# Attention phase of a one-core decoder layer: scaling of A's queries on VectorE, late stores, sample queries and sample transposes traced later, sample stream weighted 315 for 280

## The chip, the cores and the metric

The kernel is one launch on one core of a Trainium2 chip. The core has a matrix engine (PE, with its weight loads shown as PEld), a vector engine (DVE), a scalar engine (ACT) and a general engine (POOL), which run their own instruction lists in order and wait for one another by semaphores; SP only issues DMAs here, and ACT and POOL issue some too. The metric is the device time of one execution in microseconds (us); lower is better.

## What is computed

One decoder layer for a prompt of 1024 tokens and a sample group of 8 sequences with 4 new tokens each, over 1024 cached tokens in pages of 128. The reference, cut to its frame:

```python
def project(xn, w_in, pos, ...):          # one input projection, split by columns
    aq, ak, av, bq, bk, bv, iq, ik, iw = split(xn @ w_in)
    aq = rope(rms_norm(aq), pos); ak = rope(rms_norm(ak), pos)
    bq = rope(rms_norm(bq), pos); bk = rope(rms_norm(bk), pos)
...
a_out = dsa_attention(aq, iq, iw, ik, ...)   # A: 8 heads of 64, keys chosen by an indexer
b_out = diff_attention(bq, bk, bv, pos, lam) # B: 4 heads, softmax 1 - lam * softmax 2
b_out = rms_norm(b_out, subln) * (1.0 - lam_init)
h = x + concat(a_out, b_out) @ w_out
y = h + hier_moe(rms_norm(h))                # 32 experts, 2 chosen of one group of 8
```

The prompt attends to itself; the sample attends to its cached pages and its own new keys. Outputs are y for both groups and the new keys and values.

## The kernel before

The program runs in five stages, in this order: the input projection by sections of 512 columns (the last is AQ, the queries of A), with the indexer's selection among them; the head of the attention, in which the first tiles are loaded and turned; the attention; the output projection with the routing; and the experts. The prompt is cut into 8 tiles of 128 tokens, the sample is one tile of 32 rows.

**A section's end.** `evac` takes a tile's 512 columns out of PSUM. For queries and keys it copies them (ACT, `raw`), squares them, applies the rotary table (`rope`: one product on POOL, `m`, line 340, the other product and the sum on DVE, lines 342 and 343), computes the reciprocal root of the mean square (lines 348 to 352), and multiplies by it (line 387: `outs` or `outl`, by `rk`). For the query sections, prompt tiles only, line 387 is on POOL (line 386 chooses the engine); all others are on DVE. The result goes to the scratch tensor s_qa or s_qb by `store`, which keeps a few stores back in the list `late`. The last stores of AQ (tiles 6 and 7, named `outl`, two each) are still in `late` when the projection is over.

**The attention.** Two generators are interleaved by `mix`: `prompt_attention`, which goes through the 8 tiles of B and then of A, and `samples`, which does the sample's B, its A, and then the loading and splitting of w_out. Each yields the work that it has just traced as a number; `mix` always advances the one whose sum, divided by its total, is smaller. Both totals are 280. So the order on each engine is fixed by the order of tracing, and within it each engine waits for what it needs.

*Prompt.* `prep` loads a tile's keys and queries (kn, qn), splits them in two fp32r parts (kst, qh and ql), turns them (line 404), loads its values (VV, line 916) and turns its keys (line 920). For each of four pairs of heads (index u), `scores` makes the two score blocks (lines 936 and 937 on PE, 938 on DVE with the mask and the minimum, 940 the exponential on ACT), and normalises (for B lines 950, 954, 955 on DVE, which leave one block; for A line 958 on POOL). One round behind, `turned` turns the exponentials (PE line 876, then a copy `aT`), and another behind, `values` multiplies them with VV (lines 974 and 978). The list `late` is written out after tile 0 is prepared and before the loop over the tiles (lines 1039 to 1041), with `issue_after(holds[1])`, which puts the issue behind the given instruction.

*Sample.* `sample_attention` loads its queries and keys, turns them (lines 1080 and 1081, eight small transposes), clears QB on POOL (line 1083), copies the turned queries into it (line 1086, eight copies on DVE) and the keys to KN (line 1089). Then, for two groups of 4 sequences: for four chunks, it gathers 4 pages of keys (line 554, POOL), turns them (line 1104), and multiplies them with QB (line 1112); it makes the scores of the new keys (line 1120), takes the maximum, and the exponentials on ACT (line 1151 for the past, line 1152 for the new keys); it turns the exponentials (line 876 through `transposed`, from the tile sc, and line 1157), and multiplies them with 4 x 4 pages of values (line 1165). So the turn of the exponentials occurs four times: twice for B, twice for A.

After both generators, lines 1280 to 1283 split the sample's mixture mixS into a rounded part and a rest (msh, msl), which the output projection (lines 1325 to 1327) multiplies with w_out, the sample's tile first among its users.

## Time and profile before

| | |
|---|---|
| median of 3 runs | 1397.38 us (1395.25 to 1399.51) |
| the profiled execution | 1403.95 us, of it the profiled span 1402.1 us |
| PE busy in the span | 1265.0 us, 90% |
| DVE, ACT, POOL busy | 792.0 (56%), 561.5 (40%), 447.8 us (32%) |
| stage, from the span's start | projection to 466 us, head of the attention to 500 us, attention to 932 us, output projection to 1061 us, experts to 1402 us |
| PE in the output projection | 129.00 us busy of 129 |

The busy share of an engine says how much it does; which of its waits sets the end is read from the waits and the chain. In the rows further on, an instruction's line is that of the kernel before, `out<-in` are names of the program, a bracket at the end of a row is the time that the engine stood idle before it and what ended that, and PEclk is the share of full speed that the clock of PE was granted.

### The profile page before, as it was taken

The page shows a single profiled execution, that of the slowest core. Times are in us where ns is not written, and L with a number is a line of the kernel's source. Part 1 is how long each engine was busy: PE and PEld are TensorE (multiplying, and loading weights), DVE is VectorE, ACT ScalarE, POOL GpSimd, SP SyncE. Part 2 cuts the span into 40 slices and gives each one's busy share as a digit, 9 for nine tenths or more (in the row PEclk, how much of TensorE's full clock was granted, in tenths as well). Part 3 has the DMA queues.
Part 4 walks back from the last instruction along what each step waited for, and adds up shares of the span by engine and source line. Part 5 has one row for each costly group of instructions (what it writes and reads, how often), then busy time and mean ns, then how long its engine had stood idle before and what let it go on. Part 6 is the DMA issues. An engine that isn't in the chain of part 4 may idle for free.

```text
span 1402.1 us, 24778 instructions
## 1 busy us (share of the span) xinstructions
PE 1265.0 (90%) x9359; PEld 855.0 (61%) x9359; DVE 792.0 (56%) x2218; ACT 561.5 (40%) x1239; POOL 447.8 (32%) x505
## 2 busy tenths in 40 slices
PE   7999999997799689898889989999996999999994
PEld 4877675875467576776675776768884333333341
DVE  5544996969987677766655556946754111111110
ACT  5533666895432365544345555732220111111110
POOL 1012233254336534435236544321212112222101
PEclk9999999998899899999899999999997999999997
DMA  6223004133325765666467654347657999999992
GB/s 234 77 88 109 25 24 121 48 109 82 90 97 147 227 244 213 234 210 230 152 227 252 222 161 148 103 135 306 247 172 256 341 370 377 377 381 386 378 340 47
DMA packets 114149, 279.92 MB, mean 200 GB/s; under 512 B 50664, under 2 KB 50920, under 8 KB 101736
## 3 DMA queue, kind: packets, MB, share of 16 engines
q1 hardware_dynamic: 81248, 180.84, 35.4%
q0 software_dynamic: 26272, 95.43, 21.8%
q10 hardware_dynamic: 6504, 2.01, 0.6%
q8 instruction: 75, 1.23, 0.3%
q14 instruction: 50, 0.41, 0.1%
HBM read 234.33 MB, written 43.92 MB: 198 GB/s over the span
## 4 chain that ended last, share of the span: by engine, by line
PE 44%; DMA 9%; DVE 6%; issue 5%; POOL 3%; ACT 2%; SPq 0%; another core or an unknown queue 0%; POOLq 0%; ACTq 0%; DVEq 0%
PE acc L1513 9%; PE S L1533 4%; DMA wg<-in_w_exp_up_dram 4%; PE tr L1104 4%; PE tr L876 3%; PE acc L1325 3%; PE acc L1326 2%; PE acc L1327 2%; PE tr L1112 2%; PE own L1165 2%; PE acc L978 2%; DMA wg<-in_w_exp_gate_dram 2%; PE acc L974 2%; PE tr L936 2%; PE tr L937 2%
## 5 line engine op out<-in xcount | busy, mean ns | idle before, releaser
L532 PE MATMUL acc<-wh,xh 128*128 128x512 f32 x432 | 174.9, 405 | 15.3 <-ACT wh L508 15.3
L1513 PE MATMUL acc<-wg,xT 128*32 128x512 f32 x1536 | 174.7, 598 | 2.8 <-DMA wg<-in_w_exp_up_dram 2.4
L533 PE MATMUL acc<-wh,xl 128*128 128x512 f32 x432 | 172.1, 398 | 0.0
L940 ACT ACTIVATE mk<-mk,mx 128x256 f32<-128x256 f32 (+7 forms) x128 | 99.0, 775 | 83.4 <-DVE mx L938 74.0
L535 PE MATMUL acc<-wl,xh 128*128 128x512 f32 x320 | 126.6, 396 | 0.0
L1513 PEld LDWEIGHTS acc<-wg,xT 128*32 128x32 f32 x1536 | 54.6, 110 | 104.2 <-issue 95.5
L532 PEld LDWEIGHTS acc<-wh,xh 128*128 128x128 f32 x432 | 82.4, 191 | 48.0 <-ACT wh L508 25.8
L1528 DVE COPY aTe<-tr 128x256 f32<-128x256 f32 x24 | 10.2, 425 | 162.6 <-PE tr L1526 162.6
L533 PEld LDWEIGHTS acc<-wh,xl 128*128 128x128 f32 x432 | 82.5, 191 | 17.4 <-issue 1.2
L1533 PE MATMUL S<-wd,aTe 128*32 128x512 f32 x768 | 87.5, 594 | 4.3 <-DVE aTe L1528 3.3
L1508 DVE TENSOR_TENSOR xT<-tr,gc 128x512 f32<-128x512 f32 x48 | 32.9, 688 | 91.5 <-PE tr L1507 91.5
L1104 PE MATMUL tr<-cst,pg 128*128 128x128 f32 x512 | 78.8, 286 | 0.5 <-DVE ql L407 0.4
L936 PE MATMUL tr<-KS,qh 128*128 128x512 f32 (+3 forms) x192 | 75.1, 396 | 1.6 <-DVE aT L864 0.8
L1519 ACT ACTIVATE sg<-acc,its 128x256 f32<-128x256 f32 x24 | 11.4, 474 | 156.0 <-PE acc L1513 156.0
L1537 POOL DMA_INDIRECT out_o_y_dram<-yo,its x24 | 38.0, 1582 | 110.2 <-ACT yo L1536 66.1
L958 POOL TENSOR_SCALAR mk<-mk,rl 128x128 f32<-128x128 f32 (+7 forms) x64 | 49.3, 781 | 70.9 <-DVE rl L950 65.8
L1498 POOL DMA_INDIRECT xg<-s_hn,its x24 | 23.4, 977 | 142.4 <-PE tr L1507 128.9
L876 PE MATMUL tr<-cst,mk 128*128 128x128 f32 x432 | 65.1, 281 | 4.0 <-POOL mk L958 2.4
L535 PEld LDWEIGHTS acc<-wl,xh 128*128 128x128 f32 x320 | 60.9, 190 | 11.8
L937 PE MATMUL tr<-KS,ql 128*128 128x512 f32 (+3 forms) x192 | 66.2, 359 | 0.0
L1536 ACT ACTIVATE yo<-S,its 128x1024 f32<-128x1024 f32 x24 | 26.8, 1115 | 98.5 <-PE S L1533 98.5
L1104 PEld LDWEIGHTS tr<-cst,pg 128*128 128x128 f32 x512 | 61.6, 147 | 6.5 <-issue 2.0
(416 smaller groups left out, 2924.2 us busy)
## 6 DMA issues: line engine op xcount, KB each, us to landing
wg<-in_w_exp_gate_dram SPq DMA_DIRECT2D x32, 1024.0 KB
wg<-in_w_exp_up_dram SPq DMA_DIRECT2D x32, 1024.0 KB
wd<-in_w_exp_down_dram SPq DMA_DIRECT2D x32, 1024.0 KB
wr<-in_w_in_dram SPq DMA_DIRECT2D x56, 256.0 KB
xt<-in_x_prompt_dram SPq DMA_DIRECT2D x16, 512.0 KB
s_mix<-mo SPq DMA_DIRECT2D x16, 256.0 KB
qn<-s_qa SPq DMA_DIRECT2D x8, 512.0 KB
raw<-in_w_out_dram SPq DMA_DIRECT2D x16, 256.0 KB
```

The lines of the kernel that those rows point to most:

```text
L532: T_.matmul(ps, lhsT=xh[t][:, kc, :], rhs=wh[kc], start=kc == 0 and t < NT - 1, stop=False)
L533: T_.matmul(ps, lhsT=xl[t][:, kc, :], rhs=wh[kc], start=False, stop=t == NT - 1 and kc == KC - 1)
L535: T_.matmul(ps, lhsT=xh[t][:, kc, :], rhs=wl[kc], start=False, stop=kc == KC - 1)
L876: T_.transpose(pt[:, (j - b) * P:(j - b + 1) * P], src[:, j * P:(j + 1) * P], ident)
L936: T_.matmul(sp[:, :c1 - c0], lhsT=T.qh[:, h * P:(h + 1) * P], rhs=KS[:, h, c0:c1], start=True, stop=False)
L937: T_.matmul(sp[:, :c1 - c0], lhsT=T.ql[:, h * P:(h + 1) * P], rhs=KS[:, h, c0:c1], start=False, stop=True)
L940: S.activation(mk[:, :W], mk[:, :W], AF.Exp, bias=mx[:, h:h + 1], scale=-1.0, accum_out=T.ll[:, h:h + 1])
L958: G.tensor_scalar(ex[s][:, :W], ex[s][:, :W], T.rl[:, 2 * u + s:2 * u + s + 1], 1.0, op0=ALU.mult, op1=ALU.mult)
L1104: T_.transpose(pt[:, c * P:(c + 1) * P], raws[bb][:, o_:o_ + P], ident)
L1325: T_.matmul(ps[:n], lhsT=mh[:, k, :], rhs=woh[q][k], start=k == 0, stop=False)
L1513: T_.matmul(gu[c:c + m, :].rearrange("p (u f) -> p u f", u=2), lhsT=xT[:, k, c:c + m], rhs=wg[:, :, k, :], start=k == 0, stop=k == KC - 1)
L1533: T_.matmul(py[c:c + m, q * 512:(q + 1) * 512], lhsT=aT[:, k, c:c + m], rhs=wd[:, k, q * 512:(q + 1) * 512], start=k == 0, stop=k == 1)
```

## The change

- Line 387 runs on DVE for A's queries too; only BQ keeps it on POOL.
- The stores left in `late` are written out inside the loop over the tiles, when the second tile of B begins (`i == 1`), with no `issue_after`.
- The sample's queries (clearing of QB, eight small transposes, copies to QB and KN) are put into a function, called in the first group after the pages of the first chunk are turned, directly ahead of the first product with QB. In the new file the transposes are lines 1085 and 1086, the copies 1089 and 1091, the clearing 1082.
- Between the sample's exponentials and the turn of them stands `yield 7`: the prompt is traced ahead by so much before the turn is.
- The split of mixS is made at the end of `samples`, in a pool of its own, and `project` takes it from the list `ms`.
- The sample stream's total is 315 instead of 280, so it proceeds 280/315 as fast beside the prompt.

```diff
@@ evac
-            E = G if sec[1] == "Q" and t < NT else V
+            E = G if sec == "BQ" and t < NT else V
@@ prompt_attention
-        while late:
-            with tc.issue_after(holds[1]):
-                Y.dma_start(*late.pop(0))
         behind = behind2 = None
         for i in range(len(tiles)):
             cur = nxt
+
+            while i == 1 and late:
+                Y.dma_start(*late.pop(0))
@@ sample_attention
-        pt = tr()
-        for c in range(4):
-            T_.transpose(pt[:, c * NS:(c + 1) * NS], qn[:NS, c * P:(c + 1) * P], ident[:NS, :NS])
-            T_.transpose(pt[:, (4 + c) * NS:(5 + c) * NS], kn[:NS, c * P:(c + 1) * P], ident[:NS, :NS])
         QB = sp_.tile([P, 4, 8, 8, 4], F32, name="QB", bufs=1)
-        G.memset(QB, 0.0)
-        for c in range(4):
-            for s in range(2):
-                V.tensor_copy(QB[64 * s:64 * s + 64, c, :, 2 * c + s, :],
-                              pt[64 * s:64 * s + 64, c * NS:(c + 1) * NS].rearrange("p (b q) -> p b q", q=4))
         KN = sp_.tile([P, 4, NS], F32, name="KN", bufs=1)
-        V.tensor_copy(KN.rearrange("p c n -> p (c n)"), pt[:, 4 * NS:8 * NS])
+        def queries():
+            G.memset(QB, 0.0)
+            pt = tr()
...
+            V.tensor_copy(KN.rearrange("p c n -> p (c n)"), pt[:, 4 * NS:8 * NS])
@@
+                if g == 0 and ch == 0:
+                    queries()
                 sp = tr()
@@
             V.reciprocal(l2[:, 3:4], l2[:, 2:3])
+
+            yield 7
             pT = yield from transposed(ex, 8, "pT")
@@ samples
         raw.close()
+        mp = p3w.enter_context(tc.tile_pool(name="ms", bufs=1, side="right", reuse_waits="tile"))
+        msh, msl = [mp.tile([P, 8, NS], F32R, name=f"ms{u}") for u in range(2)]
+        S.copy(msh, mixS)
+        V.tensor_tensor(out=msl, in0=mixS, in1=msh.bitcast(F32), op=ALU.subtract)
+        ms.extend((msh, msl))
...
-    mix((prompt_attention("BA"), 280), (samples(), 280))
+    mix((prompt_attention("BA"), 280), (samples(), 315))
@@ project
-            mh, ml = msh, msl
+            mh, ml = ms
```

What stands in the engines' lists, before and after, at three places. The first is POOL at the end of section AQ and the head of the attention (m is the rotary product, gtab a table, kst the split keys of tile 0, pg a gathered page). Before:

```order
L387 TENSOR_TENSOR outs<-outs,rk 128x512
L340 TENSOR_TENSOR m_5056<-raw,gtab 128x512
L387 TENSOR_TENSOR outl<-outl,rk 128x512
L340 TENSOR_TENSOR m_5106<-raw,gtab 128x512
L554 DMA pg<-in_cache_b_k_dram,row_78 128x1024 x2
L387 TENSOR_TENSOR outl<-outl,rk 128x512
L1083 MEMSET QB 128x1024
L176 TENSOR_TENSOR kst<-first,kst 128x8x64
```

After:

```order
L340 TENSOR_TENSOR m_5006<-raw,gtab 128x512
L176 TENSOR_TENSOR gtab<-rot,g_4622 128x128
L340 TENSOR_TENSOR m_5056<-raw,gtab 128x512
L340 TENSOR_TENSOR m_5106<-raw,gtab 128x512
L554 DMA pg<-in_cache_b_k_dram,row_78 128x1024
L1082 MEMSET QB 128x1024
L176 TENSOR_TENSOR kst<-first,kst 128x8x64
L554 DMA pg<-in_cache_b_k_dram,row_78 128x1024 x2
```

The scalings L387 are gone from the list, one gather of a page instead of two stands ahead of kst, and the clearing of QB keeps its place ahead of kst.

The second is PE in the head of the attention, where the sample's queries are turned (`first` is the queries and keys loaded first, pg a page of the cache). Before:

```order
L1080 MATMUL tr<-cst,first 128x32
L1081 MATMUL tr<-cst,first 128x32
L1104 MATMUL tr<-cst,pg 128x128 x8
L404 MATMUL tr<-cst,first 128x128 x4
L1104 MATMUL tr<-cst,pg 128x128 x4
L920 MATMUL tr<-idr,kst 128x128 x4
```

After, further down the list:

```order
L1085 MATMUL tr<-cst,first 128x32
L1086 MATMUL tr<-cst,first 128x32
L1117 MATMUL tr<-kts,QB 32x128 x4
L936 MATMUL tr<-KS,qh 128x128
L1117 MATMUL tr<-kts,QB 32x128 x28
L937 MATMUL tr<-KS,ql 128x128
L876 MATMUL tr<-cst,mk 128x128
```

The small transposes stood ahead of all transposes of pages, with 32 products of QB some 20 rows later; they now stand directly ahead of the first product with QB, with one product of the prompt between.

The third is PE at the sample's second turn of exponentials in B (sc is the sample's tile, mk the prompt's exponentials, tile of 896 columns). Before:

```order
L1120 MATMUL tr<-KN,QB 32x32 x16
L936 MATMUL tr<-KS,qh 128x512
L937 MATMUL tr<-KS,ql 128x512
L936 MATMUL tr<-KS,qh 128x384
L937 MATMUL tr<-KS,ql 128x384
L936 MATMUL tr<-KS,qh 128x512
L937 MATMUL tr<-KS,ql 128x512
L936 MATMUL tr<-KS,qh 128x384
L937 MATMUL tr<-KS,ql 128x384
L974 MATMUL acc<-VV,aT 128x128 x6
L876 MATMUL tr<-cst,sc 128x128 x8
L1157 MATMUL tr<-cst,sc 32x128
```

After, the end of the stretch that follows L1125, the new keys' scores:

```order
L936 MATMUL tr<-KS,qh 128x512
L937 MATMUL tr<-KS,ql 128x512
L936 MATMUL tr<-KS,qh 128x384
L937 MATMUL tr<-KS,ql 128x384
L974 MATMUL acc<-VV,aT 128x128 x6
L876 MATMUL tr<-cst,mk 128x128 x7
L876 MATMUL tr<-cst,sc 128x128 x4
L404 MATMUL tr<-cst,qn 128x128 x4
L876 MATMUL tr<-cst,sc 128x128 x4
L920 MATMUL tr<-idr,kst 128x128 x4
L1164 MATMUL tr<-cst,sc 32x128
L1172 MATMUL own<-pg,pT 32x512 x8
```

Between the new keys' scores and the turn of sc stood one pair of heads of the prompt (scores, values); there are two now, with the transposes of two pairs (13 rows of L876 on mk) beside them; rows L936 to L974 of the first of them stand above the piece that is shown.

## Rows read from the trace of the kernel before

**Rows 1.** Busy time by stage: stretch, length, PE, PEld, DVE, ACT, POOL, PEclk, DMA

```profile
466.00:500.00 34.00, 19.80 (x175) 18.21 (x173) 22.09 (x75) 14.88 (x41) 15.15 (x14) 0.80 0.88 288
500.00:675.00 175.00, 152.96 (x1463) 117.67 (x1461) 123.82 (x363) 88.67 (x238) 75.37 (x74) 0.96 0.63 218
1061.00:1402.00 341.00, 300.75 (x2590) 115.21 (x2588) 62.06 (x151) 40.02 (x52) 62.85 (x52) 0.94 0.91 330
```

**Rows 2.** Waits of PE, 465 to 945 us: total, times, longest

```profile
PE tr L876 <- ACT sc L1151: 11.6, 4, 5.0
...
PE tr L920 <- ACT le L1034: 7.2, 1, 7.2
PE tr L404 <- DMA qn<-s_qb: 4.9, 1, 4.9
...
PE acc L1325 <- ACT msh L1282: 1.0, 1, 1.0
```

**Rows 3.** Timeline of POOL, end of section AQ; start, duration, idle before

```profile
466.91 1.04 POOL L387 TENSOR_TENSOR outl<-outl,rk 128x512 f32<-128x512 f32 x1 [2.45 <-DVE rk L385]
467.91 1.26 POOL L340 TENSOR_TENSOR m<-raw,gtab 128x512 f32<-128x512 f32 x1
```

**Rows 4.** Timeline of SP, the first late store and the load behind it

```profile
467.98 0.51 SPq L1041 DMA_DIRECT2D s_qa<-outl  x1
468.59 0.62 SPq L916 DMA_DIRECT2D VV<-out_o_bv_dram  x1
```

**Rows 5.** Chain that ended last, 455 to 500 us: start, duration, what

```profile
473.38 11.65 DMA qn<-s_qb
```

**Rows 6.** Timeline of PE, the four turns of the sample's exponentials

```profile
542.27 0.66 PE L876 MATMUL tr<-cst,sc 128*128 128x128 f32 x4 [0.89 <-ACT sc L1151]
...
634.38 0.90 PE L876 MATMUL tr<-cst,sc 128*128 128x128 f32 x3 [2.58 <-ACT sc L1151]
...
734.38 0.90 PE L876 MATMUL tr<-cst,sc 128*128 128x128 f32 x3 [5.00 <-ACT sc L1151]
...
832.19 1.11 PE L876 MATMUL tr<-cst,sc 128*128 128x128 f32 x4 [3.17 <-ACT sc L1151]
```

**Rows 7.** Busy time in stretches of 4 us behind three of these turns

```profile
636.00:640.00 4.00, 4.00 (x30) 1.94 (x29) 1.49 (x4) 0.11 (x1) 0.86 (x1) 0.84 0.17 39
...
732.00:736.00 4.00, 1.62 (x8) 1.62 (x9) 1.72 (x9) 1.55 (x4) 0.00 (x0) 0.60 0.67 249
736.00:740.00 4.00, 4.00 (x23) 2.13 (x25) 2.37 (x9) 1.46 (x5) 0.74 (x2) 0.54 0.00 0
...
832.00:836.00 4.00, 3.81 (x17) 3.41 (x17) 1.88 (x7) 1.43 (x6) 0.00 (x0) 0.60 0.00 0
```

**Rows 8.** DVE by line and shape, 500 to 675 us: busy us, mean ns

```profile
L938 DVE CUSTOM_DVE_ANT_0 mk<-tr,CB 128x512 f32<-128x512 f32 x34 | 22.9, 685 | 5.0 <-PE tr L937 2.0 <-remote 1.9 <-PE own L1165 1.1
...
L864 DVE COPY aT<-tr 128x512 f32<-128x512 f32 x8 | 5.5, 686 | 7.9 <-remote 3.8 <-PE own L1165 2.1 <-PE tr L876 2.0
...
L938 DVE CUSTOM_DVE_ANT_0 mk<-tr,CB,mx 128x384 f32<-128x384 f32 x8 | 4.8, 615 | 0.3
...
L955 DVE SCALAR_TENSOR_TENSOR mk<-mk,cc 128x896 f32<-128x896 f32 x4 | 4.6, 1149 | 0.1
```

**Rows 9.** Timeline of PE, one pair of heads of 896 columns at full clock

```profile
639.76 0.47 PE L936 MATMUL tr<-KS,qh 128*128 128x512 f32 x1
...
641.48 1.50 PE L974 MATMUL acc<-VV,aT 128*128 128x128 f32 x12
```

**Rows 10.** Copies to QB: duration in ns, smallest, median, largest

```profile
L1086 DVE COPY QB<-tr x16: 172/194/1264, 474.0 to 679.2; 64x32 f32<-64x32 f32 x16
```

**Rows 11.** The second rotary product on DVE, line 342, the same columns

```profile
L342 DVE TENSOR_TENSOR raw<-raw,gtab x36: 670/681/1806, 138.5 to 469.2; 128x512 f32<-128x512 f32 x32, 32x512 f32<-32x512 f32 x4
```

**Rows 12.** Timeline of POOL and DVE, one place where both ran

```profile
436.68 1.06 POOL L387 TENSOR_TENSOR outs<-outs,rk 128x512 f32<-128x512 f32 x1
...
436.71 1.58 DVE L342 TENSOR_TENSOR raw<-raw,gtab 128x512 f32<-128x512 f32 x1
```

More of the change, by code (lines that the diff above doesn't have):

```diff
@@ L1077, in sample_attention @@
         Y.dma_start(vn, vd[att][r0:r0 + NS])
-        pt = tr()
-        for c in range(4):
-            T_.transpose(pt[:, c * NS:(c + 1) * NS], qn[:NS, c * P:(c + 1) * P], ident[:NS, :NS])
-            T_.transpose(pt[:, (4 + c) * NS:(5 + c) * NS], kn[:NS, c * P:(c + 1) * P], ident[:NS, :NS])
         QB = sp_.tile([P, 4, 8, 8, 4], F32, name="QB", bufs=1)
-        G.memset(QB, 0.0)
-        for c in range(4):
-            for s in range(2):
-                V.tensor_copy(QB[64 * s:64 * s + 64, c, :, 2 * c + s, :],
-                              pt[64 * s:64 * s + 64, c * NS:(c + 1) * NS].rearrange("p (b q) -> p b q", q=4))
-        KN = sp_.tile([P, 4, NS], F32, name="KN", bufs=1)
-        V.tensor_copy(KN.rearrange("p c n -> p (c n)"), pt[:, 4 * NS:8 * NS])
+        KN = sp_.tile([P, 4, NS], F32, name="KN", bufs=1)
+        def queries():
+            G.memset(QB, 0.0)
+            pt = tr()
+            for c in range(4):
+                T_.transpose(pt[:, c * NS:(c + 1) * NS], qn[:NS, c * P:(c + 1) * P], ident[:NS, :NS])
+                T_.transpose(pt[:, (4 + c) * NS:(5 + c) * NS], kn[:NS, c * P:(c + 1) * P], ident[:NS, :NS])
+            for c in range(4):
+                for s in range(2):
+                    V.tensor_copy(QB[64 * s:64 * s + 64, c, :, 2 * c + s, :],
+                                  pt[64 * s:64 * s + 64, c * NS:(c + 1) * NS].rearrange("p (b q) -> p b q", q=4))
+            V.tensor_copy(KN.rearrange("p c n -> p (c n)"), pt[:, 4 * NS:8 * NS])
         kc_, vc_ = pages(att, "k"), pages(att, "v")
@@ L1202, in build @@
     p3w = ExitStack()
-    woh, wol = [], []
+    woh, wol, ms = [], [], []
     def samples():
@@ L1279, in build @@
     sm = p3.enter_context(tc.tile_pool(name="sm", bufs=2, reuse_waits="tile"))
-    msh = sm.tile([P, 8, NS], F32R, name="msh", bufs=1)
-    msl = sm.tile([P, 8, NS], F32R, name="msl", bufs=1)
-    S.copy(msh, mixS)
-    V.tensor_tensor(out=msl, in0=mixS, in1=msh.bitcast(F32), op=ALU.subtract)
     ovi = cq.tile([P, NT + 1, 2], I32, name="ovi")
```

## The prediction

> **What bounds the kernel now.** I read the busy time by stage first, then PE's waits in the attention, then the timelines around the waits. In the attention PE is the engine nearest to full: 152.96 of 175 us, while DVE has 123.82 [rows 1]. In its head, 466 to 500 us, PE works only 19.80 of 34 us. Behind the attention the output projection is full of PE work (table of times), and the experts stream weights with the DMA engines at 0.91 [rows 1]. Their weights are loaded into room that the attention holds, so an attention that ends earlier by some time brings the whole rest forward by it. I therefore count at the end of the attention and carry the sum over one for one.
>
> PE's waits there name the places that the edits touch [rows 2]: 11.6 us in four waits for the sample's exponentials (line 1151), 7.2 us at the first turn of keys, 4.9 us for the load of qn, 1.0 us at the output projection for msh.
>
> All terms are made against the profiled execution, 1403.95 us, which is its span of 1402.1 and 1.85 around it. It lies 6.57 us above the median, 1397.38; I take the same saving off both.
>
> **A. Scaling of A's queries on DVE, late stores.** In the list of POOL a scaling stands ahead of the next tile's rotary product. It waited 2.45 us for DVE's reciprocal root and ran from 466.91 for 1.04; only then came the product of the last tile, at 467.91 [rows 3]. Its input comes from the last products of the projection, which end as that stage does, at 466, so without the scaling POOL is free for it. On SP the first late store goes out at 467.98, just as that scaling ends [rows 4]; the root was ready at 466.91 and would itself come earlier, since the products of all tiles move up. I put the first store 2.4 us earlier, the 2.45 that the scaling waited. In SP's list one load of VV fewer stands ahead of qn's load; one issue is 0.62 [rows 4]. So qn's load is issued 3.0 us earlier; it took 11.65 from its issue at 473.38 [rows 5] and PE waited 4.9 for it [rows 2]. The 7.2 us wait also shrinks, by the scaling and the gather that no longer stand ahead of kst, but it is followed by the wait for qn, so it counts only through that. **A = -3.0**. Bounds: 0, if the DMA engines, at 0.88 in this stretch [rows 1], keep qn where it is; -5.5, if the queue is shorter by that much too. What the stores gain by leaving `issue_after` is nothing: in SP's list they stand at the same place, behind the first VV loads, and wait for DVE where they waited for POOL. The eight scalings on DVE, some 0.68 us each by line 342's like shape [rows 11], hide behind PE's section AQ, except the last, which delays only stores.
>
> A price that speaks against this part: DVE's product of line 342 takes 681 ns as a rule and 1806 at most [rows 11]; in one such place it took 1.58 us while POOL's scaling of 1.06 us began 0.03 earlier [rows 12]. The Trainium skill, page "SBUF — State Buffer", section "Who interferes with whom", says that a DVE instruction with two inputs in SBUF contends with a GpSimd instruction that reads SBUF, and whichever issues first blocks the other for its whole length. The trace agrees with it here, by the 1.58 against 0.681. By that rule each moved scaling can be held by a POOL product, 0.9 us as in rows 12; two on the way to the last store make A -1.2 and the total 1388.9.
>
> **B. The sample's queries later.** The clearing of QB and the small transposes cost nothing new. But the copies to QB, eight of 194 ns, 1.55 us [rows 10], now have PE waiting: the transposes stand directly ahead of the products with QB. Before, DVE did them while PE had other work, and PE's waits show none. Behind the waiting product in PE's list are the prompt's scores, so DVE, which gets its next work from them, can't fill the gap. This happens twice, once for B and once for A. 2 x 1.55, less the little that the one product between them hides: **B = +3.0**. Bounds: 0 (in the head other work of DVE may overlap the late qn) to +7 (DVE's queue ahead of the copies holds the prompt's normalisation too, one of 1.149 us [rows 8] each time, and some splits).
>
> **C. Turn of the exponentials 7 units later.** Removed: waits of 0.89, 2.58, 5.00 and 3.17 us [rows 6], 11.6 together. Behind three of them the granted clock of PE is low: 0.84 over 4 us after the second, 0.60 and 0.54 after the third, 0.60 after the fourth [rows 7]. What PE lost to that is its busy time by the share missing: 4.00 x 0.16 = 0.6; 1.62 x 0.40 + 4.00 x 0.46 = 2.5; 3.81 x 0.40 = 1.5. If the engine doesn't stand still before, this goes too: 4.6 in all.
>
> Against it stands that the prompt is traced alone for longer. The list shows two pairs of heads of 896 columns where one stood. A pair costs PE eight score products in 1.72 us (639.76 to 641.48), six of values in 0.75 (half of 1.50) [rows 9], and seven transposes, up to 0.165 each by the four in 0.66 [rows 6]: 3.6. It costs DVE 2 x (0.685 + 0.615) + 1.149 + 0.686 = 4.4 [rows 8], with the reads of accumulators and small operations some 5 (an estimate). So alone the prompt is bound by DVE, and the added pair costs 1.5 more than PE's work. That PE work itself is not new: it is missing in the parts with keys and values, whose 39.2 units of the sample now take 39.2 x 280/315 = 34.8 of the prompt, 4.4 fewer; there PE has the sample's products to do as well and DVE has slack. So for the two turns in B: -0.9 + 1.5 = +0.6 and -2.6 - 0.6 + 1.5 = -1.7. In A the normalisation is on POOL, and a pair is near balance: the fourth gives -3.2 - 1.5 = -4.7. The third falls into the first tiles of A, of 128 and 256 columns, where each small step passes through five engines; no row of before shows them alone. Bounds for that: 0 extra, or all of the 7.5 gained. I take half, 4.0, since two or three heads are in flight: -5.0 - 2.5 + 4.0 = -3.5. **C = 0.6 - 1.7 - 4.7 - 3.5 = -9.3**, bounds -16.2 (nothing for the prompt alone) and -1.
>
> **D. Split of mixS.** The wait of 1.0 us at the start of the output projection [rows 2] goes: the split is traced with the last of w_out's. **D = -1.0**, bounds 0 and -1.
>
> **E.** The stream of the sample ends later, by 10 us or so, and the split of w_out with it. I cost it at nothing, as the prompt's last tile covers it; if the cover is gone, PE waits for the last pieces of w_out, up to +3.
>
> Sum: -3.0 + 3.0 - 9.3 - 1.0 = -10.3. That is 1393.65 for the profiled execution, and 1397.38 - 10.3 = **1387.1** for the median.
>
> **Rivals.**
> *All waits go and the prompt alone costs nothing.* C is -16.2: -3.0 + 3.0 - 16.2 - 1.0 = -17.2, 1380.2; with A at -5.5, 1377.7. For it: DVE's queue has a lead at the start of each stretch. Against it: DVE's 4.4 to 5 over 3.6 [rows 8, 9].
> *The waits only move.* PE waits for DVE in the longer stretches as it waited for ACT, and the clock falls as before: C about -2, sum -3.0, 1394.4. For it: DVE already stands idle 5.0 and 7.9 us ahead of lines 938 and 864 (512 columns) in the window of 175 us [rows 8], mostly for PE's work, so the two engines wait for one another.
> *Slower.* The parts with keys and values don't get shorter when the prompt's share in them falls, because they go at the pace of page gathers and of the copies out of PSUM. Then the four added pairs are paid in full, 4 x 5 = 20, with 4.0 for the small tiles, against 16.2 gained: +7.8, and with the rest -3.0 + 3.0 - 1.0 the sum is +6.8, 1404.2. It decides from the point at which a part with keys and values shortens by less than 1.7 us a time (6.8 / 4). Against it: PE is busy 152.96 of 175 us there [rows 1], and hardly waits for pages.
> *The late stores do not do what they say:* their place on SP stays, as counted in A; if the DVE wait there brings nothing either, A is 0 and the sum -7.3, 1390.1, inside the forecast's case.
>
> **How the numbers follow.** Forecast 0.50, 1383 to 1392 by half of the bounds of B and C. All waits gone 0.20, 1377 to 1383. Waits only move 0.18, 1392 to 1399. Slower 0.12, 1400 to 1408. Range 1377 to 1400, which leaves the last case and a little of the second out. 0.3% is 4.2 us, about what a measurement of this kernel tells from no change: 1393.2 to 1401.6. Faster: 0.50 + 0.20 and a bit of the third case, 0.72; the same: the rest of the third and the near end of the last, 0.16; slower 0.12.
>
> **What would show it.** In the new trace, A: the last L340 of AQ near 466 and qn's wait ending near 482. B: a wait of PE at L1117 for DVE's QB copies, twice, some 1.5 us. C: no wait of PE for line 1151's successor; instead waits for DVE (lines 938, 955, aT) or POOL between L1125 and the turn of sc, and a granted clock above 0.8 behind the turns. D: no wait at the first product of the output projection. The attention should end at about 921 for 931. If B's waits are above 3 us each, or if the waits in the stretches of C exceed the 11.6 that they replace, the forecast is wrong.

## The result, and the profile after

The changed kernel takes **1405.53 us** (1402.60 to 1406.97, 6 runs) where the kernel before took 1395.62 beside it (1393.59 to 1399.51, 6 runs). The ratio is 1.0066, with a 95% interval of 1.0049 to 1.0083: some 9 us slower. The prediction was 1387.1, faster, with a range to 1400; it was wrong in the sign.

The profiled execution of after took 1406.97 us, its span is 1405.2. The one of before, on which the prediction's sum was made, was long for its kernel: 1403.95 against a median of 1395.62. So the two spans differ by only 3.1 us where the times differ by 9.9; single executions are compared below for what stands where, not for the last microseconds.

Part of what the prediction looked for in the trace of after did come. The head of the attention is shorter. POOL, then SP, then PE in their timelines (start, duration, idle before), against [rows 3 to 5]:

```profile
465.00 1.28 POOL L340 TENSOR_TENSOR m<-raw,gtab 128x512 f32<-128x512 f32 x1 [4.20 <-issue]
```

```profile
463.91 0.51 SPq L1043 DMA_DIRECT2D s_qa<-outl  x1
...
468.72 1.09 SPq L903 DMA_DIRECT2D qn<-s_qb  x1
```

```profile
477.23 1.09 PE L404 MATMUL tr<-cst,qn 128*128 128x128 f32 x4 [1.71 <-DMA qn<-s_qb]
...
482.85 0.43 PE L1117 MATMUL tr<-kts,QB 128*32 128x128 f32 x8 [1.54 <-DVE QB L1089]
```

The last product of the rotary table is at 465.00 for 467.91, the first late store at 463.91 for 467.98, and qn's load issues at 468.72 for 473.38. It then has landed before 477.23; before, it landed at 485.03. PE waits 1.54 us for the copies to QB, as priced; the second time, at 681.23, it stands 1.04 us while DVE makes them. And no wait of PE is left for the sample's exponentials, nor for msh. But the first product of the output projection starts at 935.73, where it started at 931.83 before and the prediction looked for some 921. PE's longest waits now, from 465 to 945 us, are these (total, times, longest), against [rows 2]:

```profile
PE tr L1117 <- issue: 14.1, 28, 1.1
PE acc L974 <- DVE bo L997: 4.8, 3, 3.1
PE acc L978 <- ACT aT L862: 3.8, 2, 2.2
PE tr L920 <- POOL kst L176: 3.7, 1, 3.7
PE tr L876 <- DVE mk L955: 3.5, 4, 2.2
```

The first of them is the one to read. L1117 is the product of the sample's keys with QB, 1024 small products of 32 rows in 16 runs of 64, and "issue" means that PE waited for nothing that the profile shows. Here is one such run in PE's timeline:

```profile
783.40 1.29 PE L1117 MATMUL tr<-kts,QB 128*32 128x128 f32 x39
784.89 0.45 PE L1117 MATMUL tr<-kts,QB 128*32 128x128 f32 x5 [0.19 <-issue]
785.63 0.42 PE L1117 MATMUL tr<-kts,QB 128*32 128x128 f32 x5 [0.29 <-issue]
786.35 0.27 PE L1117 MATMUL tr<-kts,QB 128*32 128x128 f32 x1 [0.30 <-issue]
787.06 0.42 PE L1117 MATMUL tr<-kts,QB 128*32 128x128 f32 x4 [0.44 <-issue]
788.48 0.43 PE L1117 MATMUL tr<-kts,QB 128*32 128x128 f32 x4 [1.00 <-issue]
789.90 0.45 PE L1117 MATMUL tr<-kts,QB 128*32 128x128 f32 x6 [0.99 <-issue]
```

The first 39 products take 1.29 us. Then they come in small pieces whose starts are 0.72 us apart, or twice that (785.63, 786.35, 787.06; 788.48, 789.90), and the run takes 6.95 us; a run without a break takes 1.95. Part of what is lost so stands under "busy", since the short products that trickle in overlap nothing. So I measure it as PE's time in these products and its idle time before them, less 16 runs of 1.95, 31.2, and call that **the excess**. By these two lines (busy, mean ns, idle before; before, then after) it is 23.2 us in the trace of before and 33.4 in that of after, of which some 2.5 are the waits for the copies to QB:

```profile
L1112 PE MATMUL tr<-kts,QB 128*32 128x128 f32 x1024 | 42.6, 276 | 11.8 <-issue 10.8 <-DVE kts L864 0.6 <-ACT kts L862 0.2
```

```profile
L1117 PE MATMUL tr<-kts,QB 128*32 128x128 f32 x1024 | 46.7, 285 | 17.9 <-issue 14.1 <-DVE QB L1089 1.5 <-PE tr L1086 1.0
```

The expectations further on give the excess as summed from the pieces of the timeline, which overlap a little; those figures differ from these by about 1 us.

The view that [rows 2] is from had this line too, its second largest, where L1112 is the same product in the kernel before:

```profile
PE tr L1112 <- issue: 10.8, 20, 1.0
```

The prediction passed over it.

The clock is the second point. Busy time in stretches of 4 us behind the third turn, of after, against the same place in [rows 7]:

```profile
724.00:728.00 4.00, 2.67 (x14) 2.00 (x15) 2.82 (x13) 3.23 (x11) 2.00 (x3) 0.72 1.00 396
728.00:732.00 4.00, 4.00 (x20) 3.15 (x18) 2.99 (x11) 1.75 (x4) 0.72 (x2) 0.50 0.42 136
732.00:736.00 4.00, 4.00 (x23) 3.18 (x19) 1.69 (x14) 3.83 (x15) 0.67 (x2) 0.50 0.17 68
736.00:740.00 4.00, 3.38 (x16) 2.55 (x17) 1.59 (x8) 2.45 (x8) 0.77 (x3) 0.50 0.17 66
740.00:744.00 4.00, 4.00 (x27) 3.45 (x25) 2.27 (x8) 2.28 (x7) 2.42 (x4) 0.64 0.17 38
```

The third turn's wait of 5.00 us is gone, but for some 20 us PE runs at half clock or little more, on the small tiles of A. By busy time times the missing share, as in the prediction, these five lose 7.9 us; before, the turn lost 2.5. The prediction looked for a granted clock above 0.8 behind the turns.

### The profile page after: what moved, and what is told of

Read it like the earlier page. It is cut to its first block, busy times and chain, and to the rows that moved or that the text cites. A ratio compares the mean times of both kernels' runs of the same rounds, so it can differ in the third digit from the quotient of the medians.

```text
span 1405.2 us, 24784 instructions
## 1 busy us (share of the span) xinstructions
PE 1276.0 (91%) x9359; PEld 861.4 (61%) x9359; DVE 797.3 (57%) x2226; ACT 560.3 (40%) x1239; POOL 441.4 (31%) x497
## 3 DMA queue, kind: packets, MB, share of 16 engines
q8 instruction: 75, 1.23, 0.4%
## 4 chain that ended last, share of the span: by engine, by line
PE 45%; DMA 10%; DVE 7%; issue 5%; POOL 2%; ACT 2%; SPq 0%; another core or an unknown queue 0%; POOLq 0%; DVEq 0%; ACTq 0%
PE acc L1522 9%; PE S L1542 4%; DMA wg<-in_w_exp_up_dram 4%; PE tr L1107 4%; PE acc L1334 2%; PE tr L876 2%; PE tr L1117 2%; PE acc L1336 2%; PE acc L1335 2%; DMA wg<-in_w_exp_gate_dram 2%; PE acc L978 2%; PE acc L974 2%; PE own L1172 1%; PE tr L937 1%; PE tr L936 1%
## 5 line engine op out<-in xcount | busy, mean ns | idle before, releaser
L940 ACT ACTIVATE mk<-mk,mx 128x256 f32<-128x256 f32 (+7 forms) x128 | 98.7, 772 | 81.5 <-DVE mx L938 75.1
L533 PEld LDWEIGHTS acc<-wh,xl 128*128 128x128 f32 x432 | 82.5, 191 | 17.3 <-issue 1.2
L936 PE MATMUL tr<-KS,qh 128*128 128x512 f32 (+3 forms) x192 | 75.2, 395 | 1.7 <-ACT KS L862 0.8
L864 DVE COPY aT<-tr 128x512 f32<-128x512 f32 (+3 forms) x87 | 46.4, 550 | 51.8 <-PE tr L876 43.1
L876 PE MATMUL tr<-cst,mk 128*128 128x128 f32 x432 | 66.1, 285 | 6.4 <-DVE mk L955 3.5
L1546 POOL DMA_INDIRECT out_o_y_dram<-yo,its x24 | 37.9, 1581 | 107.5 <-ACT yo L1545 65.5
L535 PEld LDWEIGHTS acc<-wl,xh 128*128 128x128 f32 x320 | 61.0, 191 | 11.7
```

The lines of the kernel that those rows point to most:

```text
L533: T_.matmul(ps, lhsT=xl[t][:, kc, :], rhs=wh[kc], start=False, stop=t == NT - 1 and kc == KC - 1)
L535: T_.matmul(ps, lhsT=xh[t][:, kc, :], rhs=wl[kc], start=False, stop=kc == KC - 1)
L864: V.tensor_copy(out, in_)
L876: T_.transpose(pt[:, (j - b) * P:(j - b + 1) * P], src[:, j * P:(j + 1) * P], ident)
L936: T_.matmul(sp[:, :c1 - c0], lhsT=T.qh[:, h * P:(h + 1) * P], rhs=KS[:, h, c0:c1], start=True, stop=False)
L940: S.activation(mk[:, :W], mk[:, :W], AF.Exp, bias=mx[:, h:h + 1], scale=-1.0, accum_out=T.ll[:, h:h + 1])
```

## The experiments

The runs fell on five chips, and the result was measured in a session of its own. The kernel before isn't equally quick in all of them: 1373.9, 1373.7 and 1373.8 us on three chips, 1401.6 and 1395.3 on the other two, and 1395.6 beside the result. I call them **chips at 1374** and **chips at 1396**, the result's among the latter. This was not known ahead of the first runs, and it became the main line. Each chip was met in one session only, so what is put down to a chip below could also belong to its session. Every comparison is with the kernel before on the same chip; a difference in us is the ratio's distance from 1 times before's median there. The theory at the start (T) was that the turn of the exponentials, moved behind more of the prompt, costs the time; rivals were the head (A) and the queries (B).

**The kernel before once more** (nothing changed).

> The kernel before, unchanged, for a second profile beside its times. The profiled execution of before took 1403.95 us, 8 us above its median of 1395.62. Theory H (the head of the attention in that one execution was unusual: qn's load took 11.65 us and PE waited 7.2 and 4.9 us): here the load takes less, PE's first product with QB comes earlier than 491.26, and the span is nearer to 1394. Rival (a profiled execution is about as long as that in any case): the same waits within 1 us and a span near 1402. Time 1395 by both.

1373.0 against 1373.9: ratio 0.9988 (0.9974 to 1.0003). Its profiled execution took 1373.19. The head is much as in the first trace: qn is turned at 482.96 where it was 485.16. The waits are those of the first trace within 1 us, as the rival had it; the time, which both put at 1395, is that of another chip. In PE's waits there is no issue wait before L1112, and these products cost 35.3 us in all, where the chip of the result showed 42.6 and 11.8 of idle time. By line (busy, mean ns, idle before), 465 to 940 us:

```profile
L1112 PE MATMUL tr<-kts,QB 128*32 128x128 f32 x1024 | 35.3, 275 | 0.9 <-DVE kts L864 0.8
```

The excess is 5.0 us.

**A alone.** Same chip, at 1374.

```diff
-            E = G if sec[1] == "Q" and t < NT else V
+            E = G if sec == "BQ" and t < NT else V
...
+            while i == 1 and late:
+                Y.dma_start(*late.pop(0))
```

> Before with A alone: line 387 of section AQ on DVE, late stores inside the tile loop. Theory T (the turn of the sample's exponentials, moved behind more of the prompt, costs the time) expects -3 to 0 here, 1392 to 1396. Theory A (the gain of the head in the trace of after, qn there 7.9 us earlier, is no gain beside the usual execution, and the scaling on DVE costs): 0 to +4.

1369.67: ratio 0.9974 (0.9956 to 0.9992), -3.6 us. The head's gain is real and about the -3.0 of the prediction.

**B alone.** Same chip.

```diff
...
+                if g == 0 and ch == 0:
+                    queries()
                 sp = tr()
```

> Before with B alone: the sample's queries turned and copied directly ahead of the first product with QB. Theory T expects +1 to +3 (PE waits 1.5 us for the copies twice). Theory B (the later queries are what costs, since they also move all pages' products in the list): +6 to +10, and the first product with QB late by several us.

1377.47: ratio 1.0023 (1.0007 to 1.0038), +3.2 us. The prediction had +3.0; theory B falls. The trace doesn't show the price where the prediction put it: PE waits for the copies to QB once, 0.8 us, and not twice 1.55; the second time, products of the prompt cover them. (That execution took 1373.95, 3.5 below its kernel's median.)

**C alone.** Same chip.

```diff
+            yield 7
             pT = yield from transposed(ex, 8, "pT")
...
-    mix((prompt_attention("BA"), 280), (samples(), 280))
+    mix((prompt_attention("BA"), 280), (samples(), 315))
```

> Before with C alone: 7 units between the exponentials and their turn, and the sample's total 315. Theory T expects +6 to +12, with no wait for line 1151, a lower granted clock from 720 to 745 us (0.5 to 0.7) and the third turn some 7 us later than before. Theory B expects -9 to 0 here.

1369.31: ratio 0.9965 (0.9950 to 0.9981), -4.8 us. Theory T, as I had it, fell with this: on this chip the part is a gain. The four waits for line 1151, 11.9 us there, are gone. But more than half of that time came back under other names, 4.6 of it in three: POOL's normalisation ahead of line 876 went from 2.4 to 4.0 us, `bo` ahead of line 974 from 1.9 to 3.8, line 955 ahead of 876 from 2.3 to 3.4; PE's idle time in the attention fell only from 42.9 to 38.5. And what PE lost to the clock rose from 10.7 to 14.8 (busy time times the missing share, over stretches of 4 us). These readings are of one execution, which took 1372.67, 3.4 above its kernel's median; but the clock's part recurs: e5, e7 and e19, which have C too, lose 14.0 to 15.5 there, e2 and e3 10.6 and 10.7.

Only B made the kernel slower here, and nothing so far showed a loss of 9 us. The issue waits were the one thing that I saw differ between the chips, so a new theory (I): these waits are the loss.

**The changed kernel on another chip, at 1374.**

> The changed kernel, unchanged. In the pair of the result PE stood for 'issue' before products with QB, 14.1 us in 28 waits against 10.8 in 20 before, and these products were busy 46.7 us against 42.6; in the second profile of before (another chip) there is no such wait and 35.3 us busy. Theory I (the loss comes from that supply of instructions to PE, which depends on the chip): where the kernel before shows none of it, the changed kernel is faster, by the parts measured alone -4.2 + 3.6 - 4.6 - 1.0 = -6; where it shows it, slower by 7 to 12. Rival O (the parts don't add up; together they cost time on any chip): slower by 5 or more here too, without issue waits.

1370.85 against 1373.7: ratio 0.9988 (0.9974 to 1.0003), -1.6 us, where theory I had -6. No issue wait; the excess is 7.8, of which 2.0 are the waits for the copies to QB. So the loss of 9 us is not there on this chip; a gain isn't clear either, by the interval.

**Without C** (A, B and D remain; the diff of C taken back). Same chip.

> The changed kernel without the 7 units and with the total at 280: scaling, late stores, later queries and the early split remain. Sum of the parts: -4.2 + 3.6 - 1.0 = about -2 against before. Theory I: about 4 slower than the changed kernel where there are no issue waits, 0 to 8 faster than it where there are. Rival O: faster than the changed kernel by 8 or more anywhere.

1372.59: 0.9995 (0.9983 to 1.0006), -0.7 us; 1.7 above the changed kernel, where theory I had 4.

**Without B** (the queries at their old place). Same chip.

> The changed kernel with the sample's queries at their old place. Sum of the parts: -4.2 - 4.6 - 1.0 = about -10 against before, the best version if they add up. Theory I: where there are issue waits, it has as many as the changed kernel and gains only the 3 us or so of the queries. Rival O: no better than before.

1364.81: 0.9933 (0.9912 to 0.9954), **-9.2 us**. A, C and D together make 9.2 of the 13.3 us that the prediction gave them; the queries cost 6 us inside the change, by the medians 1370.85 and 1364.81, twice what they cost alone.

**The 7 units alone, the total left at 280.** Same chip.

> Before with the 7 units alone, total still 280. The four waits of 11.9 us go as with the total at 315. If the total matters (K and V parts of the sample with fewer prompt pieces), this is slower than the turn part's -4.6, near -2; if only the wait matters, it is the same, -4 to -6.

1380.37: 1.0058 (1.0039 to 1.0078), +8.0 us, where -6 to -2 was expected. The waits for line 1151 are gone here too. But the sample's stream, with 28 units more and no more of the turn-taking, ends after the prompt, and the output projection waits for it; of PE's waits:

```profile
PE tr L1001 <- DVE bo L997: 6.7, 4, 2.9
PE acc L1327 <- ACT msh L1284: 6.7, 1, 6.7
...
PE tr L1201 <- DVE bo L1198: 5.6, 1, 5.6
```

So the total of 315 is half of part C: it is what makes room for the 7 units. The total of 315 without the 7 units (run e12) has no time: so written, the program deadlocks.

**The changed kernel on a chip at 1396** (before there 1401.61).

> The changed kernel once more, for the chip that this call meets. On two chips the kernel before took 1373.9 and 1373.7 us with no issue wait before products with QB; on the chip of the result it took 1395.6 with 10.8 us of them. Theory I: if before takes some 1395 here, issue waits are back and the changed kernel is 7 to 12 slower; if some 1374, it is 0 to 4 faster with none. Rival O (the result's loss was of that one session and not of the chip's pace): 0 to 4 faster wherever.

1405.02: 1.0023 (1.0004 to 1.0042), +3.2 us. The issue waits are back, 18.9 us of them, and the excess is 34.1, near the 33.4 of the first trace. The loss is smaller than in the result, and than the 7 to 12 of theory I. The kernel before has no profile on this chip, so its own excess there isn't known.

**Without B, and B with C alone**, both on that chip.

> The changed kernel with the queries at their old place, once more. It took 9 us less than before, the changed kernel 2 less. Theory Q (the later queries cost about 7 inside this change, twice what they cost alone): again 5 to 9 below the changed kernel. Rival (chance of one session): within 3 of it.

> Before with the turn part (7 units, total 315) and the later queries, without scaling, late stores and early split. The turn alone gave -4.8, the queries alone +3.2. If they add up: -1 to -2. Theory Q (they cost twice beside the faster sample stream, since its pages' products are then closer to what bounds it): +1 to +4.

Without B: 1402.30, 1.0008 (0.9992 to 1.0023), +1.1 us where it was -9.2 on a chip at 1374; excess 33.8. The queries cost 2.7 here (1405.02 less 1402.30), and not twice their price alone. Turn and queries without A and D: 1411.01, 1.0064 (1.0042 to 1.0086), +9.0, more than either theory had; excess 34.6. All three have the turn part, and all three have nearly the same excess, in most runs of 64 too: the thirteenth is 5.0, 5.5, 5.4 and 5.4 us too long in after's first trace, e9, e10 and e11, the fourth 0.5, 0.6, 0.6 and 0.5. So most of the waits belong to the place in the program, not to the execution.

**The kernel before, and C alone, on one chip at 1396** (before there 1395.32).

> The kernel before, for its profile on the chip of this call. Per 64 products with QB, what they take above 1.95 us sums to 23.6 us in the first trace of before (a chip at 1396) and 5.4 on a chip at 1374; the changed kernel has 34.4 and 35.1 on two chips at 1396 and 1402, 6.5 at 1374. Theory I: the sum goes with the chip's pace: some 24 if before takes 1395 or more, some 5 if it takes 1374. Rival: on a slow chip it varies by execution, anywhere from 15 to 35.

> Before with the turn part alone (7 units, total 315): -4.8 on a chip without issue waits. Theory I (the turn part packs the places where instructions run out, so its excess at the products with QB is some 34 for 24): +3 to +6 where before takes 1395 or more, -5 where it takes 1374. Rival O: -5 on any chip.

The kernel before: 1395.42, 0.9998 (0.9988 to 1.0008). C alone: 1407.01, 1.0086 (1.0063 to 1.0109), **+12.0 us**, where it was -4.8 on a chip at 1374; theory I had +3 to +6. Of PE's waits, 465 to 940 us, before and then with C:

```profile
PE tr L876 <- ACT sc L1151: 12.5, 4, 5.1
PE tr L1112 <- issue: 8.9, 22, 1.0
```

```profile
PE tr L1112 <- issue: 14.4, 32, 1.1
...
PE acc L974 <- DVE bo L997: 4.4, 3, 2.8
PE tr L876 <- DVE mk L955: 3.4, 3, 2.2
```

By line, in the same order, the products with QB and the turn of the sample's exponentials:

```profile
L1112 PE MATMUL tr<-kts,QB 128*32 128x128 f32 x1024 | 42.0, 276 | 9.2 <-issue 8.9 <-DVE kts L864 0.3
...
L876 PE MATMUL tr<-cst,sc 128*128 128x128 f32 x32 | 6.7, 354 | 12.5 <-ACT sc L1151 12.5
```

```profile
L1112 PE MATMUL tr<-kts,QB 128*32 128x128 f32 x1024 | 47.0, 278 | 15.9 <-issue 14.4 <-ACT mk L940 0.5 <-DVE ql L407 0.5
...
L876 PE MATMUL tr<-cst,sc 128*128 128x128 f32 x32 | 4.9, 275 | 0.1
```

The waits for the exponentials are gone, 12.5 us, and the excess rose by 11.7, from 20.0 to 31.7; the loss to the clock rose by 3.5 (17.3 to 20.8). PE's idle time is the same, 54.0 and 53.9. The output projection starts 10.3 us later in the second trace (934.67 for 924.39). Of this the products with QB make +11.7 and the turn, busy and idle, -14.2, so everything else, PE's work and its waits, made +12.8.

The traces of e1 and e4, the same pair on a chip at 1374, tell which of these belongs to the chip. Theirs are 35.3 and 0.9 for the products (shown at e1), 6.5 and 11.9 for the turn, and with C:

```profile
L1112 PE MATMUL tr<-kts,QB 128*32 128x128 f32 x1024 | 34.5, 275 | 0.6 <-ACT kts L862 0.5 <-DVE kts L864 0.2
...
L876 PE MATMUL tr<-cst,sc 128*128 128x128 f32 x32 | 5.5, 299 | 0.1
```

There the output projection starts 0.3 us later with C (900.98 for 900.64): the products make -1.1, the turn -12.8, everything else +14.2. So the gain at the turn and the cost elsewhere are much the same on both chips, and what differs, by 12.8 us, is the products with QB. These are single executions; by the medians C differs by 16.8 between the chips.

**The runs of 64 cut into 32.** To see whether the long runs are the cause, each is cut in two with some of the prompt between, in before and in the changed kernel without B, on the same chip:

```diff
-                sp = tr()
                 for r in range(2):
+                    sp = tr()
...
+                    S.copy(sc[:, ch * 256 + r * P:ch * 256 + (r + 1) * P], sp[:, :P])
+                    if r == 0:
+                        yield 1.1
...
```

> Before with each run of 64 products with QB cut into two of 32, with 1.1 units of the prompt between (and a second copy of 128 columns each). Theory I (PE runs out of instructions after some 30 to 48 products in a row): on a slow chip the excess falls from 24 to under 12 and the time by 8 or more; on a fast one 0 to +4 for the 16 added copies. Rival (the supply is short everywhere, and the stall moves to other lines): the excess falls, but the time stays within 3 on a slow chip.

> The changed kernel with the queries at their old place and the same cut into 32. Without the cut: -9 on a fast chip, +1 on a slow one with an excess of 34.6. Theory I: -10 or better on a slow chip, -9 to -5 on a fast one. Rival: on a slow chip within 3 of what it was without the cut.

In before: 1394.90, 0.9999 (0.9989 to 1.0010). The issue waits fell from 8.9 to 2.6 and the products from 42.0 to 37.9, and the time did not move; other waits took their place (line 1151: 13.5 for 12.5). The rival, not theory I, had this. In the changed kernel without B: 1379.74, 0.9880 (0.9860 to 0.9901), **-16.7 us**, where without the cut the same version was +1.1 on the other chip at 1396. By line, cut, in before and in the changed kernel without B:

```profile
L1112 PE MATMUL tr<-kts,QB 128*32 128x128 f32 x1024 | 37.9, 276 | 4.3 <-issue 2.6 <-ACT sc L1114 1.2 <-DVE ql L407 0.3
```

```profile
L1111 PE MATMUL tr<-kts,QB 128*32 128x128 f32 x1024 | 41.1, 281 | 5.5 <-issue 5.0 <-ACT sc L1113 0.3
```

By products and issue waits together the cut took away 10.4 us in before (50.9 to 40.5) and 17.2 in the changed kernel without B (63.3 to 46.1, e10 and e16). In before none of it reached the end, in the other all of it. That the waits for the exponentials, which stand behind these products in before alone, cover the one and not the other fits this; it was not tried by itself.

The granted clock went two ways as well. Its median over all executions is 0.962 in before on this chip (19 of them) and 0.9575 with the cut (10); it is 0.9615 in e10 (10) and 0.968 in e16 (4). In their traces PE lost to it 17.3 and then 19.2 us in the attention in the one case, 20.7 and then 10.4 in the other. That the clock alone is the gain is unlikely: in the traces with the cut at 1374 (the last three runs further on) the loss is halved as well, 14.8 and 15.4 in e4 and e7 to 7.8 and 8.4, and the times stay. But whether it only follows the supply of products or is a cause beside it, no run separates.

On one and the same chip, C alone was +12.0 (e14) and C with A, D and the cut -16.7 (e16). A and D took off 3.6 alone and 1.0 by the prediction, so some 24 us of this step are left for the cut (an estimate).

**The last three, on one more chip, at 1374** (before there 1373.8): C with the cut, the best version again, and the changed kernel.

> Before with the turn part (7 units, total 315) and the runs of 64 products cut into 32. On a slow chip the turn part alone was +12 and the cut alone 0. Theory I (the turn part loses by the issue waits at these products, and gains elsewhere): with the cut -5 to -10 on a slow chip, so the cut is worth 17 or more there; on a fast chip -5 to 0. Rival O: the turn part costs 12 with the cut as well.

> The changed kernel with the queries at their old place and the cut, once more: -15.6 on a slow chip. -10 to -16 on a slow one again; on a fast one, where it was -9 without the cut and the cut has no waits to remove, -9 to -5.

> The changed kernel on the chip of this call, beside the two with the cut: +3 to +10 where before takes 1395 or more, 0 to -4 where it takes 1374.

C with the cut: 1369.37, 0.9963 (0.9944 to 0.9982), -5.1. A, C and D with the cut: 1363.52, 0.9927 (0.9905 to 0.9949), -10.0. The changed kernel: 1370.93, 0.9980 (0.9961 to 0.9999), -2.7. With no issue waits to remove, the cut changes nothing (-5.1 for -4.8, -10.0 for -9.2), and costs nothing. In the changed kernel here the run that trickled above goes through; PE's timeline:

```profile
781.63 1.29 PE L1117 MATMUL tr<-kts,QB 128*32 128x128 f32 x38
782.85 0.50 PE L936 MATMUL tr<-KS,qh 128*128 128x512 f32 x1
783.28 1.06 PE L1117 MATMUL tr<-kts,QB 128*32 128x128 f32 x26
```

The run that was to decide whether C with the cut is a gain on a chip at 1396 met a chip at 1374, so that point rests on e16, which has A and D in it as well.

The best version is therefore the change without its later queries and with the cut: -10.0 us on a chip at 1374 and -16.7 on one at 1396, in one session each. That is faster than the kernel before on both; the changed kernel ran beside it on the first alone (1370.93 there).

## Why the prediction was wrong, by its own steps

All differences in us; the parts were timed alone or left out.

| part | predicted | chips at 1374 | chips at 1396 |
|---|---|---|---|
| A, scaling and late stores | -3.0 | -3.6 | not alone |
| B, queries later | +3.0 | +3.2 alone, 6 inside | 2.7 inside |
| C, turn later, total 315 | -9.3 | -4.8 | +12.0 |
| D, split of mixS | -1.0 | wait gone, not timed alone | wait gone |
| all | -10.3 | -1.6, -2.7 | +9.2, +3.2 |

**What bounds the kernel.** The step that failed is here, in the reading of PE's waits. The view from which [rows 2] was taken showed PE waiting 10.8 us for issue ahead of the products with QB, its second largest entry, and the prediction left it out and took those products as work that goes at PE's pace. On chips at 1396 they don't: they come in pieces. Part C's estimate says of the parts with keys that there "PE has the sample's products to do as well", and moves the prompt's pairs out of them at no cost. On these chips that is where 11.7 us of new excess arose (e13, e14), nearly the 12.5 that the waits had been. That the excess is on the path in the changed kernel without B is shown by the cut (e16 beside e14 on one chip, and beside e10 on another), with what the clock gave back in it; that it is the whole of the loss is not shown: e9's chip has the excess of the result's chip and a third of its loss.

**A** was right in kind, and its -3.6 (by the interval, -6.0 to -1.1) agrees with the -3.0. The steps of the sum were not as it had them: qn's load was issued 4.7 us earlier for 3.0, and took 8.5 at most where the sum left it at 11.65. It landed some 8 us earlier in after's trace against the first one of before, but that one was late by 2 against the second. So the agreement in size is partly luck. That leaving out `issue_after` does nothing was not tried by itself. The price by the page "SBUF — State Buffer" of the Trainium skill, section "Who interferes with whom", did not fall on the scalings: on DVE's timeline those of tiles 6 and 7 took 0.69 and 0.72 us. A small step of the chain between was held instead, while POOL's split of kst ran from 468.77 for 1.27:

```profile
463.19 0.69 DVE L387 TENSOR_TENSOR outl<-outl,rk 128x512 f32<-128x512 f32 x1
...
468.28 1.80 DVE L352 SCALAR_TENSOR_TENSOR rk<-rsq 128x8 f32<-128x8 f32 x1
470.11 0.17 DVE L385 TENSOR_SCALAR rk<-rk 128x8 f32<-128x8 f32 x1
470.31 0.72 DVE L387 TENSOR_TENSOR outl<-outl,rk 128x512 f32<-128x512 f32 x1
```

Line 352 takes 0.17 us at the tile before. That agrees with the rule in kind, two inputs in SBUF beside a POOL step that reads SBUF, but not in the order: in the profile DVE's step starts 0.49 us ahead of POOL's, and is the one that is held.

**B** had the right number alone (+3.2 for +3.0), by luck as far as its trace shows: of the two waits of 1.55 us it has one of 0.8. And a part's price is not fixed: inside the change it was 6 on a chip at 1374 and 2.7 on one at 1396. In the one case the term was mis-sized by a factor of two; the two traces (e5, e7) show PE at the first product with QB 0.9 us later and at the first new keys' scores 2.5 us later, since these first 64 products then take 3.68 us at a granted clock of 0.59 instead of 1.96. In e9's trace, of the same kernel, they take 2.48 at full clock, so this belongs to an execution too.

**C** was mis-sized even where no instruction is late: -4.8 for -9.3. The waits went, but 7.5 of the 11.9 us were taken up by other waits, most of them for DVE, ACT and POOL, as the second rival said. The clock term had the wrong sign: I took 4.6 us as given back, and 4.1 more were lost. The price of 4.0 against the 7.5 gained at the third turn was too low; there, after's five stretches lose 7.9 us to the clock alone, where before's lost 2.5. The rival that ended slower had the right place, the parts with keys and values, and a wrong cause, page gathers and copies; PE's waits for pages are 1.8 us in after.

**A sentence of the change's description** was wrong too: with its total at 315 the sample's stream isn't slowed beside the prompt but favoured, since `mix` serves the one whose sum divided by its total is smaller. The numbers of the prediction used it the right way round (39.2 units beside 34.8 of the prompt). What it is for shows in e8: without it, the 7 units cost 8.0.

**D and E** went as said in after's trace: no wait at the start of the output projection, and none for w_out.

## What to carry to other kernels

Every wait of the engine that bounds a stage belongs in the sum, also one for "issue": it is time that an edit can uncover or cover. Where many small instructions stand in a row, count how long the row takes against its fastest instance; if it varies from row to row, cutting the rows apart may be worth more than the wait that one meant to remove. And a change of a few tenths of a per cent should be timed on more than one chip, and in more than one session, before its sign is believed.

## What the runs showed of the hardware

- The same program takes 1373.0 to 1373.9 us on some chips and 1395 to 1402 on others (one session each). The whole difference lies in the attention: from the first turn of the sample's queries to the output projection it took 436.0 us in e1, 461.1 in e13 and 466.9 in the first trace, while the stages before and behind are equal within 2. The products with QB account for more than half of it: an excess of 5.0 us on the one and 20.0 to 23.2 on the other, with 42.0 to 42.6 us busy for 35.3. Prompt scores are nearly the same on both (line 936, 73.5 and 75.1 us).
- On the slower chips PE gets through some 30 to 48 of these products in most runs and then receives them a few at a time, 1 to 6 every 0.72 or 1.42 us, for a part or all of the rest. Which runs break, and by how much, is much the same from one execution and chip to the next: in the two traces of before on such chips 14 of the 16 runs agree within 0.3 us, and two differ by 0.8 and 1.0.
- What holds the instructions back was not shown. The Trainium skill, page "Runtime: NRT & Kernel Launch", section "Instruction fetch mechanics", says that an engine's instructions are streamed by its own DMA queue in blocks of 16 KiB and that this is mostly hidden. The page of the profile has two queues for instructions, and of the larger (q8 instruction: 75 packets, 1.23 MB) a packet is 16.4 KB, which agrees with the size. Whose queue it is it doesn't say, no run here changed it, and no view gives the time at which a block lands.
